# Elementwise work of both scan directions ahead of the scores, and PSUM readers ordered four dense blocks behind their matmuls

## The chip, the cores and the metric

The kernel runs on one core of one Trainium2 chip. The metric is device time in microseconds (us) of one execution. "Before" is the kernel as it was, "after" the changed one.

## The reference

The program is one inference step of a bidirectional backbone over 128 context tokens and 1024 latent tokens, width 1024: a SwiGLU feed-forward half step, a token-mixing block, and a second feed-forward half step. The change lies in the mixing block, whose heart is an RWKV-7 scan per direction and head:

```python
def rwkv7_scan(r, w, k, v, kk, a, s0, reverse):
    def step(S, inp):
        r_t, w_t, k_t, v_t, kk_t, a_t = inp
        sa = jnp.einsum('bhij,bhj->bhi', S, -kk_t)
        S = (S * w_t[:, :, None, :]
             + sa[..., None] * (kk_t * a_t)[:, :, None, :]
             + v_t[..., None] * k_t[:, :, None, :])
        return S, jnp.einsum('bhij,bhj->bhi', S, r_t)
...
    kk = k_h * p['k_k'].astype(f32).reshape(H, N)
    kk = kk * lax.rsqrt(jnp.sum(kk * kk, -1, keepdims=True) + 1e-12)
...
    y = ys[0] + ys[1]
    mean = jnp.mean(y, -1, keepdims=True)
    var = jnp.var(y, -1, keepdims=True)
    y = ((y - mean) * lax.rsqrt(var + EPS_GN)).reshape(B, T, D_RWKV)
```

Beside the scan stand large projections of the same hidden state (`h @ p['w_in']`, 5632 columns wide), which the scan needs only in part: r, k and v; the rest (g, the convolution's inputs, two gates) is read after it.

## The kernel before

**Dense work.** Each projection is three tiles of 384 tokens by 128 columns. A tile is eight blocks of three matmuls (lines 740 to 742: float32 as high and low parts), all into a PSUM tile `pj` (tag "mm", two buffers). The generator `proj` yields after every block, so a "dense block" is three matmuls of 128x384. All projections from the second group of heads on stand in one generator, `filler`, of 984 blocks, that is 2952 matmuls. With the 216 matmuls of the first group there are 3168 `pj` matmuls.

**The scan.** It is cut into 18 items: for g = 0 and 1 (four heads each) eight items of latents, both directions at once, and two items of context. Item i has a `front` (`stage_b` for each direction d: loads of `ops` and `sg`, exponentials, the products `BK` and `E`, the score matmuls `scr` of line 1047 and their masks, the transposed operand `bkt`), a `solve` (a small triangular solve: mostly DVE, lines 1079 to 1109, then the matmuls `l` of line 1116 and `l64b`), and a `seq` of two steps (lines 1165 to 1199). The loop issues `front(i+1)`, `seq(i)`, `solve(i+1)` at the highest priority, and then `fill(GI)`, which takes 40 blocks from `filler`. TensorE (PE) has one queue, in program order; a list scheduler writes that order ahead of time, chain work first where it is ready.

**Side jobs.** Three lanes run beside: `stage_k` makes the normalised key kk, `stage_v` turns v, `finish` normalises the output. A job is a generator too. Its yields are counted in dense blocks (`GL` 16, `GC` 14, `GM` 6, `GF` 8), and `PB` orders its instructions behind the block (`PB.anchor`) at which it was resumed. A job's small matmul (`cps`, `kkb`, `bon`, `vt`, `gv`) writes the one PSUM buffer of tag "oc", and its reader on DVE or ACT is issued at the same resumption. Before an item is issued, `need` takes further blocks from `filler`, one by one, until the side products of that item are issued:

```python
def need(kind, g, *bs):
    while not all((kind, 2 * g + pp, b) in made for b in bs for pp in range(2)):
        fill(1)
```

When `filler` is empty, `fill` still counts, and no matmul is issued. A full `pj` tile is read on ACT (`fso`, `ccs`, `xcs`) by `evict`, called two blocks into the next tile (`k == 1`).

After the last item the branch stage (`pb`, `pa`) loads what `finish` stored.

Of the kernel before, what the change touches and what calls it, by code (L numbers as in the profile page):

```python
# [10 lines left out]
F32 = mybir.dt.float32  # L11
F32R = mybir.dt.float32r
I32 = mybir.dt.int32
AF = mybir.ActivationFunctionType
# [46 lines left out]
def body(ctx: ExitStack, tc: tile.TileContext, I: dict, y_prompt, y_sample, new_state):  # L61
# [173 lines left out]

    def rsq(ps, n, scale, eps):
        x = tiny.tile([128, 16], F32, name="nx", tag="nx")[:, :n]
        V.tensor_scalar(out=x, in0=ps[:, :n], scalar1=scale, scalar2=eps, op0=ALU.mult, op1=ALU.add)
        return newton(x, n)

    def compact(sq, n, rhs, nr, scale, eps, tag="sc", PE=PE):
# [3 lines left out]
        return rsq(ps, n * nr, scale, eps)  # L245

# [412 lines left out]
def mixer(nc, tc, pool, env):  # L659
# [68 lines left out]
    def proj(col, evac, ts=range(NT)):  # L728

        if col not in ahead:  # L730
            assert not plan or plan[0] == col
            if plan:
                fetch()
            else:
                ahead[col] = load_w(w_in[:, col:col + 128], 8, G)
        w = ahead.pop(col)
        for t in ts:
            ps = e.psp.tile([128, TW], F32, name="pj", tag="mm")
            for k, ((hi, lo), (xh, xl)) in enumerate(zip(w, hx(t))):
                PE.matmul(ps, lo, xh, start=(k == 0), stop=False)  # L740
                PE.matmul(ps, hi, xl, start=False, stop=False)  # L741
                ins = PE.matmul(ps, hi, xh, start=False, stop=(k == 7))  # L742
                clock["dense"] += 1
                if k == 0 and t == ts[0]:
                    fetch(ins)
                if k == 5 and t == ts[len(ts) > 1]:
                    for job in halves:
                        job()
                    halves.clear()
                if k == 1:  # L750
                    evict()
# [47 lines left out]
    with ExitStack() as ph:  # L799
# [6 lines left out]

        SG = [st.tile([128, 4, 65], F32, name=f"sg{d}") for d in range(2)]
        YS = st.tile([128, 256], F32, name="ys")
        YL = st.tile([128, 4, 2, 256], F32, name="yl")
        ZV = [st.tile([128, 4, 2, 128], F32, name=f"zv{i}") for i in range(4)]  # L810
        UB = [st.tile([128, 2, 128], F32, name=f"ub{i}") for i in range(2)]
        for t_ in SG:
            G.memset(t_[:, :, 0:1], 0.0)
        for t_ in UB + [YS]:
            G.memset(t_, 0.0)
        HR = [slice(0, 64), slice(64, 128)]

        GI, GF, GL, GM, GC, SG_ = 40, 8, 16, 6, 14, 2
        def job_g(p):
# [120 lines left out]


        def stage_k(p, t0, n, bon=True):

# [18 lines left out]
            yield 3  # L962
            rs = compact(a, nt, sel, 2, 1.0, 1e-12, "oc", PB)
            yield GC
            ps = ps_.tile([128, 256], F32, name="kkb", tag="oc", bufs=1)[:, :n]
            for i in range(nt):
                for h in range(2):
                    PB.matmul(ps[HR[h], i * 128:(i + 1) * 128], rs[:, 2 * i + h:2 * i + h + 1].to_broadcast([128, 64]), ident, start=True, stop=True)
            kk = a
            V.scalar_tensor_tensor(out=kk, in0=k, scalar=e.KK_[:, p:p + 1], in1=ps, op0=ALU.mult, op1=ALU.mult)  # L970
            for h, dst in enumerate(mirrored(p, 4, 1, t0, n)):
                SP.dma_start(dst, kk[HR[h]])
            made.add(("kk", p, (t0 - NCTX) // 256))
            yield 4
            ps = ps_.tile([128, 256], F32, name="bon", tag="oc", bufs=1)[:, :n]
            PB.matmul(ps, bones, b, start=True, stop=True)
            o = v
            V.tensor_tensor(out=o, in0=v, in1=ps, op=ALU.mult)
            S.activation(out=o, in_=o, func=AF.Identity, bias=gb4[:, p:p + 1])
# [3 lines left out]
        def stage_v(p, t0, n, zv):  # L983


            nb = n // 64
            while ("rkv", p) not in made:
                yield 1
            v = oload(vd[p], t0, n, "lv", PB.first)
            yield GL  # L990
            ps = ps_.tile([128, 4, 64], F32, name="vt", tag="oc", bufs=1)
            for i in range(nb):
                for h in range(2):
                    hr, kr = HR[h], HR[1 - h]
                    PB.matmul(ps[kr, i], v[hr, i * 64:i * 64 + 64], cent[hr] if t0 >= NCTX else ident[hr, hr], start=True, stop=True)
            for h in range(2):
                S.activation(out=zv[HR[1 - h], 0:nb, p % 2, HR[h]], in_=ps[HR[1 - h], 0:nb], func=AF.Copy)
            made.add(("vt", p, (t0 - NCTX) // 256))
# [14 lines left out]
        def stage_b(g, d, t0, A, it):  # L1013
# [9 lines left out]
            c3 = "p (s t) -> p s t"  # L1023
            Fd = q1.tile([128, 4, 65], F32, name="ff", tag="ff")[:, :nb]
            S.activation(out=Fd, in_=sg, func=AF.Exp, scale=-CDEC)
            Gd = q1.tile([128, 4, 65], F32, name="fl", tag="fl")[:, :nb]
            S.activation(out=Gd, in_=sg, func=AF.Exp, scale=CDEC)
            if d == 0:
# [12 lines left out]
            mk = masks[d].unsqueeze(1).to_broadcast([128, nb, 128])  # L1041
            pst, pse = (ps_.tile([128, 4, 128], F32, name="scr", tag="sc") for x in range(2))
            for i in range(nb):
                for own, ps in ((1, pst), (0, pse)):
                    for h in range(2):
                        o = h if own else 1 - h
                        PE.matmul(ps[64 * o:64 * o + 64, i], BK[64 * h:64 * h + 64, o, i * 64:i * 64 + 64], E[64 * h:64 * h + 64, s0 + i, h], start=True, stop=True)  # L1047
            V.tensor_tensor(out=TT[:, s0:s0 + nb], in0=pst[:, :nb], in1=mk, op=ALU.mult)
            for h in range(2):
                kr = slice(64 - 64 * h, 128 - 64 * h)  # L1050
                S.activation(out=E[kr, s0:s0 + nb, h], in_=pse[kr, :nb], func=AF.Copy)
                G.tensor_tensor(out=E[kr, s0:s0 + nb, h], in0=E[kr, s0:s0 + nb, h], in1=mk[kr], op=ALU.mult)
            N = A["N"][:, 0] if d == 0 else q1.tile([128, 4, 32], F32, name="nt_", tag="nt_")
            for h in range(2):
                for b_ in range(2):
                    S.activation(out=N[quad(h, b_)], in_=TT[quad(h, b_), s0:s0 + nb, 32 * b_:32 * b_ + 32], func=AF.Copy)
            if d:
                V.transpose(out=A["N"][:, 1], in_=N)
            ps = ps_.tile([128, 4, 128], F32, name="bkt", tag="sc")
            for i in range(nb):  # L1060
                for x in range(2):
                    PE.matmul(ps[HR[x], i], BK[:, x, i * 64:i * 64 + 64], ident, start=True, stop=True)
            S.activation(out=BT[:, s0:s0 + nb], in_=ps[:, :nb], func=AF.Copy)

# [142 lines left out]
        def finish(p, t0, n, y):  # L1207
# [6 lines left out]
            yo = y  # L1214
            if t0 < NCTX:
                ps = ps_.tile([128, 256], F32, name="gm", tag="oc", bufs=1)[:, :n]
                PB.matmul(ps, bones, y, start=True, stop=True)
                V.scalar_tensor_tensor(out=yc, in0=ps, scalar=-1.0 / 64, in1=y, op0=ALU.mult, op1=ALU.add)
                yo = yc
            a = q1.tile([128, 256], F32, name="ysq", tag="f4")[:, :n]  # L1220
            PB.first(S.activation(out=a, in_=yo, func=AF.Square))
            yield GM
            rs = compact(a, nt, sel, 2, 1.0 / 64, 64e-5, "oc", PB)
            yield GC
            ps = ps_.tile([128, 256], F32, name="gv", tag="oc", bufs=1)[:, :n]
# [3 lines left out]
            V.tensor_tensor(out=yc, in0=yo, in1=ps, op=ALU.mult)  # L1229
            V.scalar_tensor_tensor(out=yc, in0=yc, scalar=gg4[:, p:p + 1], in1=bv, op0=ALU.mult, op1=ALU.add)  # L1230
# [292 lines left out]
```

## Time and profile before

| | us |
|---|---|
| median of 3 runs | 3232.46 (3229.34 to 3234.77) |
| profiled execution, its own time | 3226.22 |
| span of that execution (first to last instruction) | 3224.3 |
| mean granted TensorE clock | 0.962 |

The rows below come from the profiled execution. Its span lacks 1.9 us that lie around it, and its time is 6.2 us under the median of the runs. Feed-forward and projections fill roughly the first 1080 us and the last 1070 us; the scan with its beginnings and its tail lies between.

### The profile page before, as it was taken

What the parts mean: (1) busy time and instruction counts of PE and PEld (TensorE: products, weight loads), DVE (VectorE), ACT (ScalarE), POOL (GpSimd) and SP (SyncE); (2) the same over time, 40 slices, a digit from 0 to 9 for tenths busy, and PEclk for the clock granted to TensorE, in tenths of its full rate; (3) what the DMA queues carried; (4) which work ended last, traced back from release to release, by engine and by line L of the source; (5) the groups of instructions that cost most, each with busy time, mean ns of one, the idle gap of its engine ahead of it and who ended that gap; (6) DMA issues with size and microseconds to landing.
All of it is one profiled execution on the core that took longest, in us unless ns stands there. A gap on an engine that the chain in (4) does not pass through costs nothing.

```text
span 3224.3 us, 55042 instructions
## 1 busy us (share of the span) xinstructions
PE 3005.2 (93%) x21284; PEld 2836.3 (88%) x21284; DVE 1821.8 (57%) x4148; ACT 1151.7 (36%) x2618; POOL 453.8 (14%) x436
## 2 busy tenths in 40 slices
PE   8999999999989989988898898679989999999998
PEld 5999999999979987877777777469989999999998
DVE  7535655654875344566875668665782323323356
ACT  5421121113545424354544445332543111121244
POOL 1000000000241121333322322100220000000012
PEclk9999999999989999999999999779989999999999
DMA  8422333324534542322333223236432111111244
GB/s 271 148 63 85 111 89 92 99 79 126 163 118 133 178 132 66 111 81 79 90 114 105 88 86 108 62 112 190 141 99 66 46 38 49 46 38 45 84 144 131
DMA packets 483898, 330.80 MB, mean 103 GB/s; under 512 B 49768, under 2 KB 461748, under 8 KB 483636
## 3 DMA queue, kind: packets, MB, share of 16 engines
q1 hardware_dynamic: 483008, 326.80, 33.9%
q8 instruction: 167, 2.74, 0.4%
q14 instruction: 95, 0.78, 0.1%
q10 hardware_dynamic: 308, 0.44, 0.0%
q0 software_dynamic: 320, 0.04, 0.0%
HBM read 265.58 MB, written 61.60 MB: 101 GB/s over the span
## 4 chain that ended last, share of the span: by engine, by line
PE 69%; DVE 17%; ACT 5%; issue 4%; DMA 3%; POOL 1%; SPq 0%; DVEq 0%; ACTq 0%; POOLq 0%
PE po L220 6%; PE po L219 6%; PE po L221 6%; PE pg L220 5%; PE pg L219 5%; PE pg L221 5%; PE pu L220 5%; PE pu L219 5%; PE pu L221 5%; PE pj L742 3%; PE pj L740 3%; PE pj L741 3%; DVE un L1088 2%; PE scr L1047 2%; DMA ops<-opd 1%
## 5 line engine op out<-in xcount | busy, mean ns | idle before, releaser
L138 ACT ACTIVATE whi<-wst 128x512 fp32r<-128x512 f32 (+1 forms) x578 | 350.4, 611 | 731.6 <-PE po L221 393.1
L139 DVE TENSOR_TENSOR wlo<-wst,whi 128x512 fp32r<-128x512 f32 (+1 forms) x480 | 326.7, 681 | 305.4 <-ACT whi L138 296.1
L740 PE MATMUL pj<-hh,wlo 128*128 128x384 f32 x1056 | 375.4, 355 | 0.3 <-ACT fso L768 0.3
L741 PE MATMUL pj<-hl,whi 128*128 128x384 f32 x1056 | 371.1, 351 | 2.7 <-POOL hl L269 1.4
L742 PE MATMUL pj<-hh,whi 128*128 128x384 f32 x1056 | 371.3, 352 | 0.0
L220 PE MATMUL pg<-hl,whi 128*128 128x384 f32 x1056 | 356.8, 338 | 5.3 <-POOL hl L269 2.9
L219 PE MATMUL po<-ah,wlo 128*128 128x384 f32 x1056 | 357.1, 339 | 3.8 <-ACT ah L138 3.8
L219 PE MATMUL pg<-hh,wlo 128*128 128x384 f32 x1056 | 357.7, 339 | 1.9 <-DVE wlo L139 1.3
L220 PE MATMUL po<-al,whi 128*128 128x384 f32 x1056 | 356.3, 338 | 0.4 <-DVE al L139 0.4
L221 PE MATMUL pg<-hh,whi 128*128 128x384 f32 x1056 | 356.1, 337 | 0.0
L221 PE MATMUL po<-ah,whi 128*128 128x384 f32 x1056 | 355.7, 337 | 0.0
L219 PE MATMUL pu<-hh,wlo 128*128 128x384 f32 x1056 | 355.4, 337 | 0.0
L220 PE MATMUL pu<-hl,whi 128*128 128x384 f32 x1056 | 354.0, 335 | 0.0
L221 PE MATMUL pu<-hh,whi 128*128 128x384 f32 x1056 | 354.0, 335 | 0.0
L279 POOL TENSOR_TENSOR ss<-ss,sqt 128x384 f32<-128x384 f32 x78 | 88.7, 1140 | 1695.8 <-ACT sqt L278 1691.3
L432 DVE TENSOR_TENSOR sil<-sil,pu 128x384 f32<-128x384 f32 x132 | 72.8, 552 | 352.7 <-PE pu L221 352.6
L404 DVE TENSOR_TENSOR o<-o,po 128x384 f32<-128x384 f32 x288 | 159.0, 552 | 172.4 <-PE po L221 171.4
L741 PEld LDWEIGHTS pj<-hl,whi 128*128 128x128 f32 x1056 | 204.3, 193 | 9.9 <-issue 3.0
L740 PEld LDWEIGHTS pj<-hh,wlo 128*128 128x128 f32 x1056 | 203.7, 193 | 10.4 <-issue 5.7
L742 PEld LDWEIGHTS pj<-hh,whi 128*128 128x128 f32 x1056 | 204.2, 193 | 7.4 <-issue 3.3
L220 PEld LDWEIGHTS pg<-hl,whi 128*128 128x128 f32 x1056 | 200.1, 189 | 7.8 <-DVE hl L271 3.9
L219 PEld LDWEIGHTS po<-ah,wlo 128*128 128x128 f32 x1056 | 198.6, 188 | 4.8 <-ACT ah L138 4.8
(584 smaller groups left out, 5746.9 us busy)
## 6 DMA issues: line engine op xcount, KB each, us to landing
wst<-in_ffn_w SPq DMA_DIRECT2D x324, 256.0 KB, 2.9
wmod<-in_w_mod SPq DMA_DIRECT2D x144, 256.0 KB, 2.8
wst<-in_w_in SPq DMA_DIRECT2D x94, 256.0 KB, 3.3
ops<-opd SPq DMA_DIRECT2D x36, 640.0 KB, 4.5
wst<-in_ffn_w SPq DMA_DIRECT2D x96, 192.0 KB, 2.5
xo<-xd SPq DMA_DIRECT2D x64, 192.0 KB, 3.9
wst<-in_w_out SPq DMA_DIRECT2D x48, 256.0 KB, 2.8
opd<-zv SPq DMA_DIRECT2D x24, 384.0 KB, 2.8
```

The source lines that it names most:

```text
L138: first(S.activation(out=hi, in_=src, func=AF.Copy))
L139: eng.tensor_tensor(out=lo, in0=src, in1=hi.bitcast(F32), op=ALU.subtract)
L219: PE.matmul(ps, lo, xh, start=(k == 0), stop=False)
L220: PE.matmul(ps, hi, xl, start=False, stop=False)
L221: later.tick(PE.matmul(ps, hi, xh, start=False, stop=(k == nk - 1)))
L279: eng.tensor_tensor(out=ssum, in0=ssum, in1=q, op=ALU.add)
L404: V.tensor_tensor(out=O[m][t], in0=O[m][t], in1=ps, op=ALU.add)
L432: V.tensor_tensor(out=s, in0=s, in1=pu, op=ALU.mult)
L740: PE.matmul(ps, lo, xh, start=(k == 0), stop=False)
L741: PE.matmul(ps, hi, xl, start=False, stop=False)
L742: ins = PE.matmul(ps, hi, xh, start=False, stop=(k == 7))
L1047: PE.matmul(ps[64 * o:64 * o + 64, i], BK[64 * h:64 * h + 64, o, i * 64:i * 64 + 64], E[64 * h:64 * h + 64, s0 + i, h], start=True, stop=True)
```

## The change

Four edits. (1) `stage_b` is split: it does the loads, exponentials and products of its direction and returns `scores`; `front` calls both directions' first parts and then both `scores`. The buffers `ff` and `fl`, shared by the directions, go: one exponential is written to a static tile per direction (`sf`), the other in place over `sg`, whose first column is now 1 instead of 0. (2) In the side jobs the reader of a small matmul is issued four yields (`GV`) after it, and ordered behind the block reached by then. (3) `take` holds the "oc" buffer for one job at a time, from the matmul to its reader; a job that finds it held comes back 7 blocks later. (4) `evict` is called four blocks into the next tile (`k == 3`).

```diff
-                if k == 1:
+                if k == 3:
                     evict()
...
+        SF = [st.tile([128, 4, 65], F32, name=f"sf{d}") for d in range(2)]
...
-        for t_ in SG:
-            G.memset(t_[:, :, 0:1], 0.0)
+        for t_ in SG + SF:
+            G.memset(t_[:, :, 0:1], 1.0)
...
-        GI, GF, GL, GM, GC, SG_ = 40, 8, 16, 6, 14, 2
+        GI, GF, GL, GM, GC, SG_, GV = 40, 8, 16, 6, 14, 2, 4
...
+        held = []
+        def take():
+            while held:
+                yield 7
+            held.append(1)
+
         def stage_k(p, t0, n, bon=True):
...
-            rs = compact(a, nt, sel, 2, 1.0, 1e-12, "oc", PB)
+            yield from take()
+            ps = e.sums(a, nt, sel, 2, "oc", PB)
+            yield GV
+            rs = e.rsq(ps, 2 * nt, 1.0, 1e-12, PB.first)
+            held.clear()
             yield GC
+            yield from take()
             ps = ps_.tile([128, 256], F32, name="kkb", tag="oc", bufs=1)[:, :n]
...
-            V.scalar_tensor_tensor(out=kk, in0=k, scalar=e.KK_[:, p:p + 1], in1=ps, op0=ALU.mult, op1=ALU.mult)
+            yield GV
+            PB.first(V.scalar_tensor_tensor(out=kk, in0=k, scalar=e.KK_[:, p:p + 1], in1=ps, op0=ALU.mult, op1=ALU.mult))
+            held.clear()
...
-            Fd = q1.tile([128, 4, 65], F32, name="ff", tag="ff")[:, :nb]
-            S.activation(out=Fd, in_=sg, func=AF.Exp, scale=-CDEC)
-            Gd = q1.tile([128, 4, 65], F32, name="fl", tag="fl")[:, :nb]
-            S.activation(out=Gd, in_=sg, func=AF.Exp, scale=CDEC)
+            Fd, Gd = SF[d], sg
+            S.activation(out=Fd[:, :, 1:65], in_=sg[:, :, 1:65], func=AF.Exp, scale=-CDEC)
+            S.activation(out=Gd[:, :, 1:65], in_=sg[:, :, 1:65], func=AF.Exp, scale=CDEC)
...
-            if g < 2:
-                stage_b(g, 0, NCTX + j * 128, A[i], i)
-                stage_b(g, 1, NCTX + (7 - j) * 128, A[i], i)
-            else:
-                for d in range(2):
-                    stage_b(j, d, 0, A[i], i)
+            at = [(g, NCTX + j * 128), (g, NCTX + (7 - j) * 128)] if g < 2 else [(j, 0)] * 2
+            for f in [stage_b(gg, d, t0, A[i], i) for d, (gg, t0) in enumerate(at)]:
+                f()
```

`bon`, `vt`, `gv` and the sums of `finish` get the same `take`, `yield GV` and `PB.first`.

What this does to the order of the `pj` matmuls can be counted. `need` takes 170, 140, 0 and 50 blocks ahead of items 0, 2, 9 and 10 in the kernel before, and 229, 198, 60 and 130 in the changed one; everywhere else `fill(GI)` takes its 40. In the written order of PE, so many of the 3168 `pj` matmuls stand ahead of the end of each item's `l` matmuls:

| item | 0 | 1 | 2 | 3 | 4 | 5 | 6 | 7 | 8 | 9 | 10 | 11 | 12 | 13 | 14 | 15 | 16 | 17 |
|---|---|---|---|---|---|---|---|---|---|---|---|---|---|---|---|---|---|---|
| before | 882 | 955 | 1419 | 1549 | 1668 | 1803 | 1925 | 2041 | 2150 | 2238 | 2525 | 2641 | 2756 | 2879 | 3005 | 3129 | 3168 | 3168 |
| after | 1058 | 1136 | 1780 | 1894 | 2022 | 2146 | 2263 | 2369 | 2481 | 2807 | 3168 | 3168 | 3168 | 3168 | 3168 | 3168 | 3168 | 3168 |

The first place is PE's queue around the solve of item 15 (`l`; `cps`, `gv`, `kkb`, `vt`, `bon` are side jobs' small matmuls, `yp` is the scan's step). Before:

```order
L741 MATMUL pj<-hl_1_8842,whi 128x384
L742 MATMUL pj<-hh_1_8841,whi 128x384
L1116 MATMUL l_20892<-xr,ab_20604 32x32 x2
L740 MATMUL pj<-hh_1_8867,wlo 128x384
L741 MATMUL pj<-hl_1_8868,whi 128x384
L742 MATMUL pj<-hh_1_8867,whi 128x384
L1116 MATMUL l_20892<-xr,ab_20605 32x32 x2
```

The same place of the changed kernel's PE queue, where line 1116 has become line 1144:

```order
L1205 MATMUL yp<-e_20302,zv_9437 64x64 x4
L177 MATMUL cps<-cst,ysq 128x2 x2
L177 MATMUL cps<-cst,oa 128x2
L177 MATMUL gv<-cst,ny 64x128 x4
L177 MATMUL kkb<-cst,ny 64x128 x2
L177 MATMUL vt<-cst,lv 64x64 x4
L177 MATMUL bon<-od,cst 128x128
L177 MATMUL cps<-cst,ysq 128x2 x2
L1144 MATMUL l_20580<-xr,ab_20296 32x32 x2
```

The dense matmuls that stood before and within the solve are gone from this place; small matmuls of side jobs follow each other without a block between.

The second place is DVE's queue behind the transpose that opens a solve in the middle of the scan (`un` is the solve, `ops` and `e` are the next item's products, `zv` the running step). Before:

```order
L1088 TENSOR_TENSOR un<-lm,x_14773 128x24
L1039 TENSOR_TENSOR e_15076<-ops,ff 64x4x64
L1040 TENSOR_TENSOR e_15076<-ops,ff 64x4x64
L1039 TENSOR_TENSOR e_15076<-ops,ff 64x4x64
L1040 TENSOR_TENSOR e_15076<-ops,ff 64x4x64
L1184 COPY zv_9436<-sq 64x2x64
L1184 COPY zv_9435<-sq 64x2x64
L1039 TENSOR_TENSOR e_15077<-ops,fl 64x4x64
```

And in the changed kernel:

```order
L1060 TENSOR_TENSOR ops<-ops,sf_9433 128x512
L1063 TENSOR_TENSOR e_15517<-ops,sf_9432 64x4x64
L1064 TENSOR_TENSOR e_15517<-ops,sf_9432 64x4x64
L1063 TENSOR_TENSOR e_15517<-ops,sf_9432 64x4x64
L1064 TENSOR_TENSOR e_15517<-ops,sf_9432 64x4x64
L1063 TENSOR_TENSOR e_15518<-ops,sg_9431 64x4x64
L1064 TENSOR_TENSOR e_15518<-ops,sg_9431 64x4x64
L1063 TENSOR_TENSOR e_15518<-ops,sg_9431 64x4x64
L1064 TENSOR_TENSOR e_15518<-ops,sg_9431 64x4x64
L1212 COPY zv_9438<-sq 64x2x64
```

Both kernels have the products of both directions in the same stretch of the solve; the first product now stands ahead of them and all eight stand in a row, ahead of the step's copies. The masks of the scores stand behind the solve in both kernels.

## Rows read from the trace of the kernel before

**Rows 1.** The page: busy time and share of each engine.

```profile
PE 3005.2 (93%) x21284; PEld 2836.3 (88%) x21284; DVE 1821.8 (57%) x4148; ACT 1151.7 (36%) x2618; POOL 453.8 (14%) x436
```

**Rows 2.** Windows cut at items' first L1116 instruction: each engine's busy time, clock, DMA.

```profile
core 0: us, PE busy (x) PEld busy (x) DVE busy (x) ACT busy (x) POOL busy (x), PEclk, DMA share, GB/s
1083.30:1212.10 128.80, 117.33 (x752) 110.53 (x750) 47.29 (x110) 35.33 (x78) 31.25 (x24) 0.94 0.45 131
1253.60:1371.30 117.70, 109.64 (x843) 99.96 (x842) 57.73 (x151) 41.33 (x101) 36.95 (x32) 0.94 0.36 104
...
2015.50:2054.50 39.00, 23.92 (x362) 19.73 (x362) 26.83 (x92) 14.47 (x39) 8.75 (x10) 0.85 0.33 100
2054.50:2093.10 38.60, 23.23 (x358) 18.34 (x358) 28.68 (x102) 15.74 (x47) 6.22 (x8) 0.72 0.07 21
2093.10:2156.50 63.40, 42.20 (x338) 33.21 (x338) 35.50 (x127) 20.50 (x53) 1.15 (x4) 0.67 0.33 94
...
1371.30:1662.90 291.60, 253.49 (x2845) 216.02 (x2845) 209.56 (x614) 138.27 (x383) 100.05 (x98) 0.95 0.31 90
1662.90:1788.00 125.10, 112.19 (x1147) 96.98 (x1147) 77.91 (x216) 54.81 (x152) 32.26 (x30) 0.95 0.36 104
1788.00:2093.10 305.10, 251.44 (x3036) 211.32 (x3036) 214.70 (x687) 144.65 (x417) 79.99 (x84) 0.91 0.29 86
```

**Rows 3.** The same windows, instructions that touch `pj` alone (PE, PEld, ACT).

```profile
1083.30:1212.10 128.80, 105.65 (x562) 98.69 (x562) 11.29 (x23) 0.94 0.45 131
1253.60:1371.30 117.70, 90.75 (x465) 81.18 (x464) 9.32 (x19) 0.94 0.36 104
...
2054.50:2093.10 38.60, 0.00 (x0) 0.00 (x0) 0.00 (x0) 0.72 0.07 21
...
1371.30:1662.90 291.60, 158.54 (x735) 128.81 (x735) 15.12 (x31) 0.95 0.31 90
1662.90:1788.00 125.10, 76.31 (x372) 64.03 (x372) 7.87 (x16) 0.95 0.36 104
1788.00:2093.10 305.10, 136.18 (x646) 109.88 (x646) 13.20 (x27) 0.91 0.29 86
```

**Rows 4.** A window in which PE runs `pj` matmuls alone, columns as in rows 3.

```profile
1274.90:1287.20 12.30, 12.30 (x72) 12.03 (x70) 1.48 (x3) 1.00 0.54 161
```

**Rows 5.** DVE in order of time, around the end of item 16's solve.

```profile
2054.51 0.45 DVE L1109 STREAM_TRANSPOSE xr<-xr 128x256 f32<-128x256 f32 x1
...
2059.75 0.69 DVE L1048 TENSOR_TENSOR ab<-scr,cst 128x512 f32<-128x512 f32 x1 [4.75 <-PE scr L1047]
...
2065.12 0.69 DVE L1048 TENSOR_TENSOR ab<-scr,cst 128x512 f32<-128x512 f32 x1 [2.63 <-PE scr L1047]
...
2069.27 1.25 DVE L1079 STREAM_TRANSPOSE lm<-nn 128x1024 f32<-128x1024 f32 x1
```

**Rows 6.** Waits over the whole program: us in total, times, longest us.

```profile
DVE ab L1048 <- PE scr L1047: 104.4, 30, 6.5
ACT fso L768 <- PE pj L742: 94.1, 40, 4.5
DVE nx L238 <- PE cps L177: 71.0, 30, 8.3
...
DVE oa L970 <- PE kkb L177: 36.4, 9, 5.9
...
DVE or L978 <- PE bon L177: 21.7, 11, 2.9
```

**Rows 7.** The chain that ended last, behind the last item: start, us, what.

```profile
2112.98 0.30 DVE yc__22273 L1218
...
2124.50 0.30 DVE yc__22306 L1218
...
2129.97 0.30 DVE yc__22339 L1218
...
2132.16 0.69 PE pb L220
```

More of the change, by code (lines that the diff above doesn't have):

```diff
@@ L234, in newton, with rsq, sums @@
         return y
-    def rsq(ps, n, scale, eps):
+    def rsq(ps, n, scale, eps, first=lambda ins: None):
         x = tiny.tile([128, 16], F32, name="nx", tag="nx")[:, :n]
-        V.tensor_scalar(out=x, in0=ps[:, :n], scalar1=scale, scalar2=eps, op0=ALU.mult, op1=ALU.add)
+        first(V.tensor_scalar(out=x, in0=ps[:, :n], scalar1=scale, scalar2=eps, op0=ALU.mult, op1=ALU.add))
         return newton(x, n)
-    def compact(sq, n, rhs, nr, scale, eps, tag="sc", PE=PE):
+    def sums(sq, n, rhs, nr, tag="sc", PE=PE):
         ps = psp.tile([128, 16], F32, name="cps", tag=tag, bufs=1 if tag == "oc" else 2)
@@ L244, in compact @@
             PE.matmul(ps[:, i * nr:(i + 1) * nr], sq[:, i * 128:(i + 1) * 128], rhs, start=True, stop=True)
-        return rsq(ps, n * nr, scale, eps)
+        return ps
+    def compact(sq, n, rhs, nr, scale, eps, tag="sc", PE=PE):
+        return rsq(sums(sq, n, rhs, nr, tag, PE), n * nr, scale, eps)
     def bcast(rs, sp, PE=PE):
@@ L974, in stage_k @@
             yield 4
+            yield from take()
             ps = ps_.tile([128, 256], F32, name="bon", tag="oc", bufs=1)[:, :n]
@@ L977, in stage_k @@
             o = v
-            V.tensor_tensor(out=o, in0=v, in1=ps, op=ALU.mult)
+            yield GV
+            PB.first(V.tensor_tensor(out=o, in0=v, in1=ps, op=ALU.mult))
+            held.clear()
             S.activation(out=o, in_=o, func=AF.Identity, bias=gb4[:, p:p + 1])
@@ L990, in stage_v @@
             yield GL
+            yield from take()
             ps = ps_.tile([128, 4, 64], F32, name="vt", tag="oc", bufs=1)
@@ L995, in stage_v @@
                     PB.matmul(ps[kr, i], v[hr, i * 64:i * 64 + 64], cent[hr] if t0 >= NCTX else ident[hr, hr], start=True, stop=True)
+            yield GV
             for h in range(2):
-                S.activation(out=zv[HR[1 - h], 0:nb, p % 2, HR[h]], in_=ps[HR[1 - h], 0:nb], func=AF.Copy)
+                PB.first(S.activation(out=zv[HR[1 - h], 0:nb, p % 2, HR[h]], in_=ps[HR[1 - h], 0:nb], func=AF.Copy))
+            held.clear()
             made.add(("vt", p, (t0 - NCTX) // 256))
@@ L1040, in stage_b @@
                 V.tensor_tensor(out=E[hr, s0:s0 + nb, h, 64:128], in0=r[hr].rearrange(c3, t=64), in1=fr[hr], op=ALU.mult)
[L1041 to L1063, printed above, removed]
+            def scores():
+                mk = masks[d].unsqueeze(1).to_broadcast([128, nb, 128])
+                pst, pse = (ps_.tile([128, 4, 128], F32, name="scr", tag="sc") for x in range(2))
+                for i in range(nb):
+                    for own, ps in ((1, pst), (0, pse)):
+                        for h in range(2):
+                            o = h if own else 1 - h
+                            PE.matmul(ps[64 * o:64 * o + 64, i], BK[64 * h:64 * h + 64, o, i * 64:i * 64 + 64], E[64 * h:64 * h + 64, s0 + i, h], start=True, stop=True)
+                V.tensor_tensor(out=TT[:, s0:s0 + nb], in0=pst[:, :nb], in1=mk, op=ALU.mult)
+                for h in range(2):
+                    kr = slice(64 - 64 * h, 128 - 64 * h)
+                    S.activation(out=E[kr, s0:s0 + nb, h], in_=pse[kr, :nb], func=AF.Copy)
+                    G.tensor_tensor(out=E[kr, s0:s0 + nb, h], in0=E[kr, s0:s0 + nb, h], in1=mk[kr], op=ALU.mult)
+                N = A["N"][:, 0] if d == 0 else q1.tile([128, 4, 32], F32, name="nt_", tag="nt_")
+                for h in range(2):
+                    for b_ in range(2):
+                        S.activation(out=N[quad(h, b_)], in_=TT[quad(h, b_), s0:s0 + nb, 32 * b_:32 * b_ + 32], func=AF.Copy)
+                if d:
+                    V.transpose(out=A["N"][:, 1], in_=N)
+                ps = ps_.tile([128, 4, 128], F32, name="bkt", tag="sc")
+                for i in range(nb):
+                    for x in range(2):
+                        PE.matmul(ps[HR[x], i], BK[:, x, i * 64:i * 64 + 64], ident, start=True, stop=True)
+                S.activation(out=BT[:, s0:s0 + nb], in_=ps[:, :nb], func=AF.Copy)
@@ L1065, in quad @@
+            return scores
         def quad(h, b):
@@ L1215, in finish @@
             if t0 < NCTX:
+                yield from take()
                 ps = ps_.tile([128, 256], F32, name="gm", tag="oc", bufs=1)[:, :n]
@@ L1219, in finish @@
                 yo = yc
+                held.clear()
             a = q1.tile([128, 256], F32, name="ysq", tag="f4")[:, :n]
@@ L1222, in finish @@
             yield GM
-            rs = compact(a, nt, sel, 2, 1.0 / 64, 64e-5, "oc", PB)
+            yield from take()
+            ps = e.sums(a, nt, sel, 2, "oc", PB)
+            yield GV
+            rs = e.rsq(ps, 2 * nt, 1.0 / 64, 64e-5, PB.first)
+            held.clear()
             yield GC
+            yield from take()
             ps = ps_.tile([128, 256], F32, name="gv", tag="oc", bufs=1)[:, :n]
@@ L1228, in finish @@
                     PB.matmul(ps[HR[h], i * 128:(i + 1) * 128], rs[:, 2 * i + h:2 * i + h + 1].to_broadcast([128, 64]), ident, start=True, stop=True)
-            V.tensor_tensor(out=yc, in0=yo, in1=ps, op=ALU.mult)
+            yield GV
+            PB.first(V.tensor_tensor(out=yc, in0=yo, in1=ps, op=ALU.mult))
+            held.clear()
             V.scalar_tensor_tensor(out=yc, in0=yc, scalar=gg4[:, p:p + 1], in1=bv, op0=ALU.mult, op1=ALU.add)
```

## The prediction

> **What bounds the kernel now.** I read the page first: PE is busy 93% of the span, DVE 57%, ACT 36% [rows 1]. So the program as a whole is PE's, and work that is only late on DVE or ACT costs nothing until PE waits for it. Then I cut the scan at each item's first `l` matmul and read the windows twice, for all engines and for the dense matmuls (`pj`) alone. They fall into three kinds. Where `need` pours in dense blocks, PE is nearly full: 117.3 of 128.8 us ahead of item 0, 109.6 of 117.7 us between items 1 and 2, 112.2 of 125.1 us between items 8 and 10 [rows 2]. In the ordinary items PE is busy 253.5 of 291.6 us (items 2 to 8) [rows 2], and 158.5 us of that are dense matmuls [rows 3]. At the end there is none left: from item 16 to 17 not one `pj` matmul runs [rows 3], PE is busy 23.2 of 38.6 us at a granted clock of 0.72, and DVE 28.7 us [rows 2].
>
> Compare an item with dense work and one without: items 10 to 17 take 305.1 us, 43.6 us each, and carry 646 `pj` matmuls [rows 2, 3]; the item without any takes 38.6 us [rows 2]. A dense matmul alone on PE costs 12.3 us / 71 = 0.173 us [rows 4] (the window touches 72, the first and last in part). The 92 of an item are thus 16 us of PE time, and the item is only 5 us longer for them. Dense work under the scan costs about a third of its price; beside `need` it costs all of it.
>
> **The change part by part.** *Where the blocks go.* Each reader now comes 4 blocks after its matmul, and `take` sends rivals for the buffer away for 7 blocks at a time. `need` waits for these jobs in blocks, so it takes 229, 198, 60 and 130 of them in place of 170, 140, 0 and 50, 257 more. `filler` has no more blocks than before: it now runs empty at item 10, where it ran empty at item 16. The counts of `pj` matmuls ahead of each solve, which stand with the change, give the shifts, at 0.173 us each:
>
> - ahead of item 0: 1058 for 882, 176 more: +30.4 us
> - items 0 to 1: 5 more: +0.9 us
> - items 1 to 2: 644 for 464, 180 more: +31.1 us
> - items 2 to 8: 701 for 731, 30 fewer: -5.2 us
> - items 8 to 10: 687 for 375, 312 more: +54.0 us
>
> Together +111.2 us. These stretches are PE's own (rows above), so I take the full price; the gaps that could swallow some are a term of their own below.
>
> The Trainium skill ("TensorE: Matmul & The Clock Gate", Back-to-back issue gap) gives N/2.4 + 2.5 ns for one isolated matmul at the upper clock, an estimate of 162.5 ns for 384 columns. By it the +111.2 us would be about +104 us, 7 us less; the trace's 0.173 us differs and decides.
>
> *What comes back.* Items 10 to 17 lose all their 643 matmuls. Each interval then resembles the one from item 16 to 17. The rows of its DVE show what is left: from the solve's last transpose (2054.5) to the next opening one (2069.3) are 14.8 us, with waits of 4.75 and 2.63 us for the score matmuls; the rest of the item is the solve itself, on DVE [rows 5]. I take 38 us, a little under 38.6 since evictions and weights are gone: 7 x 38 = 266 for 305.1, -39 us. Bounds: 7 x 35 = 245 (-60 us), 35 being the 38.6 less half the 7.4 us of those waits; and 43.6 as now (0 us).
>
> *Readers, evictions.* The waits aimed at are real: DVE waits 71.0 us for `cps`, 36.4 for `kkb`, 21.7 for `bon`, ACT 94.1 us for `pj` [rows 6]. But they are waits for PE, at moments when PE has other work; what they can give back is at most the time that PE stands idle. Through item 10 that is 11.5 + 8.1 + 38.1 + 12.9 = 70.6 us (the windows less their PE busy time [rows 2]). Most of it is the chain's own latency, and an ordinary item's jobs now spread over more items; I take a quarter, -18 us, bounds 0 and -71. The later eviction has two more blocks to wait, 6 x 0.173 = 1.0 us, and the second `pj` buffer covers it: a tile is 24 x 0.173 = 4.2 us, so 2.1 us are left from the fourth block to the tile's end. If that cover failed, PE would wait for ACT; no row shows such a wait now, and I take 0 (to +10 us, a tenth of ACT's 94.1 reversed).
>
> *Both directions first.* The static `sf` and `sg` remove nothing from DVE's count. The score masks wait 104.4 us for PE [rows 6], but the written order has them behind the solve before and after, so I take 0. Against it: the first product now stands before the eight others, and waits for GpSimd and the `ops` load ahead of the solve. Bounds: 0, and a gain or loss of at most one such mask wait, 3.5 us an item (104.4 / 30), which the ends above and below already span.
>
> What is queued behind the later readers: the stores of kk on SP's queue, and behind these the `ops` load of the item's `front`. They come 8 blocks later in each `stage_k` (two `GV`), which is just what `need` now waits out in blocks, so this wait is in the +111.2 us already. The in-place exponential adds one more: the next item's `sg` load on SP, with the loads and stores queued behind it, now waits for the products of the item before instead of its exponentials. These products run within the first third of the solve, an item ahead of the load's use, so the price is 0 as long as an item is some 38 us long.
>
> *The tail.* After the last item, `finish` jobs run one after another, with a single buffer for their loads. Before, four (context) are left; in the changed order three more matmul groups (`cps`, `gv`) of `finish` stand behind the last solve. Consecutive jobs start 11.5 and 5.5 us apart (2113.0, 2124.5, 2130.0), and the dense branch follows at 2132.2 [rows 7]. Three more cost 3 x 5.5 to 3 x 11.5, 16 to 35 us; part runs beside the last two steps, so I take +15, bounds +8 and +35.
>
> Sum: 111.2 - 39 - 18 + 15 = +69 us. On the profiled 3226.2 us that is 3295 us. The median of the runs stands 6.2 us above that execution; I add it: **3302 us**, 2.1% slower.
>
> **The rivals.**
>
> *B, the bare items give nothing back.* Without dense work the granted clock is 0.72 and, in the tail, 0.67 [rows 2]; side jobs stand in PE's queue back to back, so their readers wait where they are issued. If each bare item stays at 43.6 us, 39 us are not returned: 3341 us, and with the long tail 3361. For it: side work of four context keys and eight outputs falls into these items. Against: the item from 16 to 17 had the low clock already and two `finish` jobs, and took 38.6 us. The Trainium skill ("TensorE: Matmul & The Clock Gate", The HAM clock gate) has the clock at half rate after idle time; by that rule bare items stay near the lower level throughout. The granted 0.72 agrees in part only.
>
> *C, the waits were the path.* If the waits of side readers had each been on the chain, their removal would be worth 71.0 + 36.4 + 21.7 = 129 us [rows 6] in place of 18: 111.2 - 39 - 129 + 15 = -42 us, 3191 us, faster. It decides from 111.2 - 39 + 15 = 87 us of waits on the path. Against it: PE idles 70.6 us through item 10, all causes together, and the chain cannot outrun PE there.
>
> *D, nothing moves.* If the order had not changed where it counts, the time would be within 0.2% (6.5 us; runs of one kernel spread by 5.4 us, so less than that is no measurable change). The counts speak against it: the blocks are moved in the written program.
>
> **How the numbers follow.** The forecast with its neighbourhood, 3270 to 3330: 0.58. B and the long tail, 3330 to 3375: 0.22. Larger gains by short waits or bare items near 35 us, 3239 to 3270: 0.11. D: 0.03. C: 0.06. The ends of all terms together would be 3232 + 111 - 60 - 71 + 8 = 3220 and 3232 + 111 + 35 + 10 = 3388, but they are not met at once. The range 3255 to 3355 leaves out C, D, half of the small gains and the upper half of B, 2 in 10. Faster 0.06, same 0.03, slower 0.91.
>
> **What would show it.** In the profile after: the last `pj` matmul stands ahead of item 10's solve, and the windows from item 10 to 17 hold none, with a granted clock of 0.6 to 0.8 and 36 to 40 us an item; item 0's `l` comes about 25 to 30 us later and item 10's about 90 us later than now; the waits of `nx`, `oa` and `or` on PE shrink to a fraction; the stretch from the last solve to steady `pb` grows from 63 to some 75 us. I am wrong in the size of the gain if the items 2 to 8 shorten by more than 3 us each; wrong in the give-back if bare items take under 35 or over 42 us; wrong altogether if the chain reaches item 10 at today's time, which would mean that PE had room for the blocks.

## The result and the profile after

The changed kernel takes 3365.91 us (median of 4 runs, 3360.41 to 3370.67), the kernel before beside it 3233.61 us: ratio 1.041, 95% interval [1.0394, 1.0426]. It is slower by 132 us, where I had forecast 69, and stands 11 us above the top of my range. The direction and the place were right, the size was not. The profiled execution took 3360.41 us, its span is 3358.5 us.

First the page, busy time and share of each engine, answering to [rows 1]:

```profile
PE 3029.0 (90%) x21284; PEld 2869.7 (85%) x21284; DVE 1816.1 (54%) x4148; ACT 1147.5 (34%) x2618; POOL 454.5 (14%) x438
```

PE does the same 21284 matmuls; 134 us were added to the span and only 24 to PE's busy time. So PE now stands idle where it did not before. To find where, the windows cut at the items' first `l` matmul (line 1116 has become 1144), columns as in [rows 2]. They are: ahead of item 0, items 1 to 2, 2 to 8, 8 to 10, the end of that one by itself, 10 to 17, and from item 17 to the first `pb`:

```profile
1083.30:1234.10 150.80, 139.42 (x907) 133.10 (x907) 47.23 (x111) 39.43 (x87) 36.59 (x28) 0.98 0.41 118
1276.00:1431.80 155.80, 142.07 (x1036) 131.78 (x1036) 66.67 (x164) 49.66 (x119) 53.22 (x47) 0.94 0.29 85
1431.80:1705.50 273.70, 247.26 (x2722) 210.26 (x2723) 186.01 (x533) 128.29 (x363) 86.38 (x88) 0.92 0.33 94
1705.50:1917.50 212.00, 178.51 (x1568) 158.85 (x1569) 98.52 (x311) 72.24 (x191) 40.76 (x36) 0.91 0.36 108
1881.40:1917.50 36.10, 8.53 (x68) 6.09 (x70) 27.45 (x81) 7.88 (x20) 6.76 (x5) 0.53 0.50 141
1917.50:2208.20 290.70, 150.71 (x2344) 123.45 (x2345) 191.46 (x610) 118.17 (x363) 58.51 (x68) 0.61 0.15 41
2208.20:2266.30 58.10, 27.37 (x276) 20.66 (x276) 28.02 (x126) 8.69 (x31) 1.14 (x4) 0.53 0.16 46
```

The `pj` matmuls alone in four of these windows, answering to [rows 3]:

```profile
1083.30:1234.10 150.80, 129.21 (x709) 122.37 (x707) 14.19 (x29) 0.98 0.41 118
1276.00:1431.80 155.80, 122.99 (x646) 113.06 (x646) 12.72 (x26) 0.94 0.29 85
1705.50:1917.50 212.00, 136.29 (x692) 119.83 (x691) 14.12 (x29) 0.91 0.36 108
1917.50:2208.20 290.70, 0.00 (x0) 0.00 (x0) 0.00 (x0) 0.61 0.15 41
```

Against [rows 2, 3] this gives the account of the 134 us of span, beside my terms. The columns before and after are lengths of windows; the line from item 17 runs to the end of the span.

| stretch | before | after | difference | my term |
|---|---|---|---|---|
| ahead of item 0 | 128.8 | 150.8 | +22.0 | +30.4 |
| items 0 to 1 | 41.5 | 41.9 | +0.4 | +0.9 |
| items 1 to 2 | 117.7 | 155.8 | +38.1 | +31.1 |
| items 2 to 8 | 291.6 | 273.7 | -17.9 | -5.2 |
| items 8 to 10 | 125.1 | 212.0 | +86.9 | +54.0 |
| items 10 to 17 | 305.1 | 290.7 | -14.4 | -39 |
| item 17 to the end | 1131.2 | 1150.3 | +19.1 | +15 |
| waits removed, wherever | | | | -18 |

Two rows carry the miss: items 8 to 10, 33 us dearer than I had them, and items 10 to 17, which gave back 14 us for 39.

The last `pj` matmul ends at 1881.4, and item 10's `l` starts at 1917.5. In between PE is busy 8.5 of 36.1 us. The chain of waits through that stretch, in order of time (start, us, what; a few of its pieces):

```profile
1881.70 0.45 SPq L1046
1882.20 0.68 SPq L1046
1882.93 2.04 SPq L1027
1885.01 4.15 DMA f<-bvd
1889.18 1.51 DVE e L1064
1890.70 0.37 SPq L1045
1891.12 2.16 DMA sg<-opd
...
1900.55 0.42 DVE e L1063
1900.97 1.40 DVE e L1064
1902.37 0.60 DVE ops L1060
...
1916.98 0.41 DVE xr L1136
1917.45 0.43 DVE xr L1137
1917.93 0.64 PE l L1144 x28
```

The reader is to see loads on SP's queue first, then the front's products, then the solve on DVE, up to `l`: no dense matmul is left that could stand beside it. The waits of the same stretch (us in total, times, longest) name the late loads of `ops` and `sg`:

```profile
POOL ops L1059 <- DMA ops<-opd: 29.8, 3, 25.1
ACT sf L1050 <- DMA sg<-opd: 10.5, 1, 10.5
```

I had also said that the waits of `nx`, `oa` and `or` would shrink to a fraction. Over the whole program they grew, against [rows 6]:

```profile
DVE ab L1074 <- PE scr L1073: 110.3, 29, 7.2
DVE nx L238 <- PE cps L177: 89.8, 35, 11.8
DVE oa L988 <- PE kkb L177: 67.0, 10, 8.5
DVE or L999 <- PE bon L177: 35.5, 12, 4.3
```

They are no sign of time on the path. Cut by stretch, most of `oa` and `or` and much of `nx` stand ahead of item 2, where `need` pours in blocks and DVE has little else to do (the first window of these waits, after):

```profile
DVE oa L988 <- PE kkb L177: 54.8, 7, 8.5
DVE nx L238 <- PE cps L177: 40.0, 6, 11.8
...
DVE or L999 <- PE bon L177: 30.1, 8, 4.3
```

In the ordinary items 2 to 8, where I had looked for their price, the kernel before had only this:

```profile
DVE nx L238 <- PE cps L177: 3.1, 4, 1.6
DVE or L978 <- PE bon L177: 2.8, 2, 1.5
```

and the kernel after has 1.2 us of `nx` there. Rival C, which wanted 129 us of such waits on the path, had no more than 6 us in these items.

### The profile page after: what moved, and what is told of

It reads as the page before. It is cut to its first block, busy times and chain, and to the rows that moved or that the text cites. A ratio compares the mean times of both kernels' runs of the same rounds, so it can differ in the third digit from the quotient of the medians.

```text
span 3358.5 us, 55083 instructions
## 1 busy us (share of the span) xinstructions
PE 3029.0 (90%) x21284; PEld 2869.7 (85%) x21284; DVE 1816.1 (54%) x4148; ACT 1147.5 (34%) x2618; POOL 454.5 (14%) x438
## 4 chain that ended last, share of the span: by engine, by line
PE 71%; DVE 17%; ACT 4%; DMA 3%; issue 3%; POOL 2%; SPq 0%; DVEq 0%; ACTq 0%; POOLq 0%
PE po L220 6%; PE po L219 6%; PE po L221 6%; PE pg L220 5%; PE pg L221 5%; PE pg L219 5%; PE pu L220 5%; PE pu L219 5%; PE pu L221 5%; PE pj L743 4%; PE pj L744 4%; PE pj L745 4%; DVE un L1116 3%; PE scr L1073 2%; DMA ops<-opd 1%
## 5 line engine op out<-in xcount | busy, mean ns | idle before, releaser
L743 PEld LDWEIGHTS pj<-hh,wlo 128*128 128x128 f32 x1056 | 203.9, 193 | 12.9 <-issue 7.8
L219 PEld LDWEIGHTS pg<-hh,wlo 128*128 128x128 f32 x1056 | 200.4, 190 | 2.4 <-DVE wlo L139 1.6
```

## The experiments

Two theories went into the first four runs. **A**: the loss is the early use of the dense blocks, nothing else. **B**: a good part of it lies in the readers or the new front themselves. All ratios are against the kernel before on the same chip.

**e1, only the blocks taken earlier.** The kernel before, with

```diff
         need("kk", 0, 0, 3)
+        fill(229 - clock["now"])
...
+            fill(max(0, {1: 467, 8: 807, 9: 977}.get(i, 0) - clock["now"]))
             with chain():
```

> The kernel before with none of the four edits; extra dense blocks are taken ahead of items 0, 2, 9 and 10, so that as many as in the changed kernel are gone by then (229, 467, 807 and 977) and the filler runs empty at item 10. Theory A (the loss is the early use of the blocks alone): 3345 to 3370 us, first l of item 0 some 20 to 25 us later than before, no pj matmul behind about 1880 us, items 10 to 17 bare at 41 to 42 us each. Theory B (a good part of the loss is in the readers or in the front that does both directions first): clearly less than the changed kernel, under 3330 us.

Measured 3280.24 us, 1.0147 [1.0132, 1.0162]: a third of the loss. Theory A in this form fell, and the time is one that theory B allowed. The trace says why. Of `pj` matmuls 875 stand ahead of item 0's `l`, as in the kernel before (880), not 1056: the extra blocks were taken when the job that the chain waits for was already issued, so the scheduler could put the chain ahead of them. Between items 1 and 2 and between 8 and 10 the same holds in part (612 and 549 `pj` matmuls for 646 and 691). Blocks taken early cost as far as the job that is waited for stands behind them.

**e2, the readers alone** (edits 2 and 3; front, buffers and evict as before):

> The kernel before with edits 2 and 3 alone (readers four yields later, the oc buffer held); front, sf/sg and evict as before. Theory A: the same as the changed kernel, 3355 to 3375 us, since the blocks are taken as in it (229, 198, 60, 130). Theory B, in the form that the front or the later evict costs: 20 us or more under the changed kernel, 3345 us or less.

3365.49 us, 1.0406 [1.039, 1.0423]: the whole loss. The front and the later evict add none of it.

**e3, all but the readers** (edits 1 and 4):

> The changed kernel without edits 2 and 3 (no GV, no take): both directions first, sf static, sg in place, evict four blocks into the next tile; blocks are taken as in the kernel before. Theory A: no change, 3225 to 3245 us. Theory B, in the form that the front costs at item 10 (36.9 us without a dense matmul): slower, 3255 us or more. If both directions first frees PE of the score masks' waits (104.4 us over 30): faster, under 3220 us.

3218.09 us, 0.9958 [0.9944, 0.9973]: 14 us faster than before, better than either theory had it; only the side remark on the score masks' waits allowed it, and e8 does not bear that out. Both edits were at 0 in my sum.

**e4, readers four yields later, other gaps shorter by as much.** The changed kernel, with

```diff
-        GI, GF, GL, GM, GC, SG_, GV = 40, 8, 16, 6, 14, 2, 4
+        GI, GF, GL, GM, GC, SG_, GV = 40, 4, 12, 6, 10, 2, 4
...
             while held:
-                yield 7
+                yield None
...
-            if self.cur is None or clock["now"] < self.at:
+            if self.cur is None or clock["now"] < self.at or self.stuck and held:
```

where `stuck` is set by a yield of None.

> The changed kernel with its readers still four yields behind their matmuls, but with the other gaps of the jobs shortened by as much (GL 12, GC 10, GF 4) and a job that finds the oc buffer held resumed when it is free instead of 7 blocks later: 179, 146, 0 and 100 blocks are taken ahead of items 0, 2, 9 and 10 (before 170, 140, 0, 50; changed 229, 198, 60, 130), and the filler runs empty at item 14. Theory A: near the kernel before, 3230 to 3265 us. Theory B, in the form that later readers cost by themselves: 3290 us or more. If later readers give back what I summed as waits removed (18 us), under 3225 us.

3253.55 us, 1.0063 [1.0051, 1.0075], within theory A's range. So the readers stand behind four blocks and 111 of the 132 us are gone, as soon as the jobs are hardly longer (`need` takes 425 blocks, 360 before). A gain by the readers themselves does not show here.

From these four I formed **theory L**: what costs is the length of a side job, counted in blocks. In the changed kernel each `stage_k` is longer by three `GV` of 4, and by 7 for each time that it finds the buffer held. `need` waits it out with blocks that stand ahead of the chain, wherever in the job the readers are.

**e5, longer gaps, no edit at all.** The kernel before, with

```diff
-        GI, GF, GL, GM, GC, SG_ = 40, 8, 16, 6, 14, 2
+        GI, GF, GL, GM, GC, SG_ = 40, 14, 20, 22, 20, 2
```

> The kernel before with none of the four edits, but longer gaps in the side jobs (GL 20, GC 20, GF 14, GM 22 for 16, 14, 8, 6), so that need takes about as many blocks as in the changed kernel (227, 472, 800 and 973 gone ahead of items 0, 2, 9 and 10 for 229, 467, 807 and 977). Readers stand at the resumption of their matmul, as before. Theory L (what costs is the length of a side job counted in blocks, wherever its readers stand): 3350 to 3380 us, as the changed kernel. Theory R (readers behind blocks cost by themselves): 3275 to 3310 us, near the run in which only blocks were taken earlier (3280).

3373.27 us, 1.043 [1.0413, 1.0448]. The loss is reproduced with every reader at its matmul's side. Theory L holds, and its rival, that the readers cost by themselves, is out.

**e6, need counts on without blocks.** The changed kernel, with

```diff
             for _ in range(n):
-                PB.anchor = next(filler, PB.anchor)
+                if not hold:
+                    PB.anchor = next(filler, PB.anchor)
```

and `hold` set while `need` runs from item 8 on.

> The changed kernel, but from item 8 on need counts on without taking blocks from the filler, so 190 blocks stay for later: 323 pj matmuls stand between the solves of items 8 and 10 for 687, and items 11 to 14 get 363. Theory L with PE as the price of need's blocks: items 8 to 10 shorter by about 364 x 0.173 = 63 us, items 10 to 17 longer by 5 to 15 us, 3300 to 3330 us. Rival (that stretch is the side jobs' own latency, the blocks only ride along): items 8 to 10 still over 190 us, 3350 us or more.

3285.63 us, 1.0168 [1.0154, 1.0182], 80 us less than the changed kernel and more than I expected. All engines, items 8 to 10 and 10 to 17:

```profile
1708.40:1832.80 124.40, 109.66 (x1171) 92.71 (x1170) 91.06 (x288) 55.75 (x158) 33.04 (x30) 0.96 0.39 112
1832.80:2129.00 296.20, 208.54 (x2716) 172.90 (x2716) 196.67 (x628) 131.97 (x393) 69.54 (x76) 0.78 0.25 70
```

Items 8 to 10 fell from 212.0 to 124.4 us, so the blocks set that stretch and not the side jobs' own latency. Items 10 to 17 rose by 5.5 us only, although 365 of the `pj` matmuls now run in them.

**e7, no readers, gaps shorter than before.** Edits 1 and 4, with

```diff
-        GI, GF, GL, GM, GC, SG_, GV = 40, 8, 16, 6, 14, 2, 4
+        GI, GF, GL, GM, GC, SG_, GV = 40, 4, 12, 4, 10, 2, 4
```

> The changed kernel without edits 2 and 3, and with shorter gaps in the side jobs (GL 12, GC 10, GF 4, GM 4): need takes 133, 92, 0 and 0 blocks ahead of items 0, 2, 9 and 10 (before 170, 140, 0, 50), and the filler lasts past item 17. Theory L, turned round: what need does not take costs a third or less under the scan. 112, 125 and some 140 pj matmuls fewer in the three stretches are 19 + 22 + 24 = 65 us, given back at a third to a half: 3160 to 3200 us. Rival (the stretches are the side jobs' own latency): 3205 to 3225 us, as the run without edits 2 and 3 (3218). Rival (small matmuls so close behind their inputs stop PE's queue): over 3225 us.

3170.07 us, 0.9806 [0.9791, 0.9821], as theory L has it: 48 us under e3 for 135 blocks fewer taken by `need`. Items 10 to 17, all engines and then `pj` alone:

```profile
1722.30:2024.20 301.90, 273.36 (x3182) 231.77 (x3182) 217.12 (x677) 146.25 (x422) 88.41 (x90) 0.96 0.30 88
```

```profile
1722.30:2024.20 301.90, 168.87 (x792) 137.24 (x792) 16.02 (x33) 0.96 0.30 88
```

These are the rows against which the bare items of the changed kernel are to be read: 792 dense matmuls and 11.2 us more, 0.014 us each, where one alone takes 0.173 us [rows 4]. The granted clock differs too, 0.96 here for 0.61 there; the last section comes back to it.

**e8, the front alone** (edit 1):

> The kernel before with edit 1 alone (both directions first, sf static, sg in place); evict two blocks into the next tile as before. If the 14 us that edits 1 and 4 together gave back are the front's: 3212 to 3224 us. If they are the later evict's: 3228 to 3238 us. My prediction had both at nothing.

3228.00 us, 0.9986 [0.9975, 0.9997]. **e10, the later evict alone** (edit 4, `k == 3`):

> The kernel before with edit 4 alone: a full pj tile is read four blocks into the next one for two. My prediction had it at 0 to +10 us. The front alone gave 3228 us and both together 3218, so if the two add up: 3218 to 3227 us. If the later evict helps only with the new front, or the difference was chance: 3228 to 3236 us. If PE waits for ACT, as my bound has it: 3238 us or more.

3225.46 us, 0.9985 [0.9973, 0.9998]. Each gives some 5 us, with an interval that is just clear of none; multiplied they make 0.9971, at the edge of what e3 measured for both. That they help a little together is shown, which of them does more is not.

**e9, all four edits, gaps shorter.** As e4, with `GL` 10, `GC` 7, `GF` 2, `GM` 4, `GV` 2.

> All four edits, with gaps so short (GL 10, GC 7, GF 2, GM 4, GV 2, a job that finds oc held resumed when it is free) that need takes 140, 88, 0 and 0 blocks, as in the run with short gaps and no readers (133, 92, 0, 0; 3170 us); pj matmuls ahead of the solves of items 0, 2 and 17 are 788, 1182 and 2934 for 772, 1178 and 2939. Theory L (only blocks count, readers nothing): 3160 to 3185 us. If the readers' waits for PE are worth the 18 us that I summed, with the same blocks: 3155 us or less. If readers behind blocks cost by themselves: 3190 us or more.

3152.03 us, 0.9753 [0.9735, 0.9771]: 78 us faster than before, the fastest of all, and 18 us under e7 with nearly the same blocks ahead of each solve. 11 of the 18 us stand where I had looked for them, in the ordinary items: items 2 to 8 take 284.1 us for e7's 295.2, with 743 `pj` matmuls for 736 (all engines; e9, then e7):

```profile
1327.20:1611.30 284.10, 250.64 (x2879) 214.66 (x2879) 204.49 (x636) 139.38 (x385) 100.22 (x98) 0.97 0.33 95
```

```profile
1329.70:1624.90 295.20, 260.35 (x2872) 221.82 (x2872) 213.34 (x637) 137.72 (x384) 98.02 (x96) 0.92 0.32 91
```

That readers behind blocks are worth something, if the job does not grow by them, is the likely reading. It is not shown: the gaps of the two runs are not the same.

**e11, gaps shorter still, no readers.** Edits 1 and 4 with `GI` 46, `GL` 8, `GC` 6, `GF` 2, `GM` 2, `SG_` 1:

> The run with short gaps and no readers taken further: GL 8, GC 6, GF 2, GM 2, a side step after each block (SG_ 1), and GI 46 so that the filler still ends with the scan; need takes 113, 46, 0 and 0 blocks. 61 and 80 pj matmuls fewer ahead of item 0 and between items 1 and 2 are 24 us by 0.173, given back at up to a half by more blocks per item: 3145 to 3162 us by theory L. Rival (the stretches have come down to the side jobs' own latency): 3163 to 3175 us, no change from 3170. Rival (small matmuls so close behind their inputs stop PE): over 3175 us.

3160.52 us, 0.9782 [0.976, 0.9803]. In theory L's range, but its interval overlaps that of e7. Items 1 to 2 fell from 99.3 to 85.6 us; part of it went into the item from 16 to 17, which took 66.3 us with 220 `pj` matmuls. PE was busy 62.0 us of them, so cover has a bound: in an item with that many blocks PE is the limit again.

**e12, the last blocks kept for item 10.** The changed kernel, with

```diff
-                PB.anchor = next(filler, PB.anchor)
+                if not (hold and clock["now"] >= 984 - 42):
+                    PB.anchor = next(filler, PB.anchor)
```

and `hold` set while `need` runs.

> The changed kernel, but need leaves the last 42 blocks of the filler: it counts on without them ahead of item 10, and fill takes them behind item 9, so that they can stand beside the front and solve of item 10, which ran 36.9 us without a dense matmul. Blocks ahead of each solve are as many as in the changed kernel (2807 and 3168 at items 9 and 10). Theory I (part of the 87.7 us of items 8 to 10 is idle PE time beside item 10, since the filler ran empty just there): items 8 to 10 up to 42 x 3 x 0.173 = 22 us shorter, 3340 to 3355 us. Rival (items 8 to 10 cost what their blocks cost on PE, 0.173 each, wherever they stand): no change, 3360 to 3371 us.

3353.53 us, 1.0384 [1.037, 1.0398], 12 us under the changed kernel; the intervals just overlap. In its profiled execution items 8 to 10:

```profile
1711.70:1911.20 199.50, 176.60 (x1564) 157.72 (x1563) 97.51 (x297) 70.98 (x189) 40.92 (x35) 0.96 0.38 112
```

12.5 us less than in the changed kernel, with as many `pj` matmuls: PE's idle time there went from 33.5 to 22.9 us. So part of that stretch's cost was idle time beside item 10, about half of what these blocks could cover. The whole of that execution was no shorter, though: it took 3360.93 us, the slowest of its five, and the changed kernel's profiled one 3360.41. Items 10 to 17 took 6.5 us more, items 2 to 8 2.3 us more, and item 0's `l` came 3.7 us later. The gain in the stretch is shown; that it is the 12 us of the medians is not.

## Why the prediction missed the size

**What was right.** PE bounds the `need` stretches, and the shift of dense blocks ahead of the chain is the loss. Ahead of item 2 my terms sum to 62.4 us and 60.5 were measured. e5 makes the same loss with no edit, e6 takes most of it back. The last `pj` matmul stands ahead of item 10's solve, items 10 to 17 hold none, at a granted clock of 0.58 to 0.64 (0.6 to 0.8 was written down), and item 0's `l` came 22 us late for 25 to 30. Item 10's came 130 us late for 90. The tail's +15 was +19.1: more of `finish` is left behind item 17, as the chain shows, answering to [rows 7], and the first `pb` comes 59 us behind that item's `l` where it came 39 us behind it:

```profile
2225.63 0.43 DVE yc__22072 L1265
2236.58 0.49 DVE yc__22072 L1267
...
2240.57 0.40 DVE yc__22105 L1267
2267.18 0.69 PE pb L220
```

The front and the evict at 0 were small gains, 14 us together in e3; beside the long jobs they vanish (e2 against the changed kernel), and why was not tried. Two small slips of the working: the 70.6 us of idle time leave out items 0 to 1 (2.1 us), and what the range leaves out sums to a quarter, not to 2 in 10.

**One step that failed: "What comes back", -39 us, measured -14.4.** I took the item from 16 to 17, 38.6 us without dense work, for what items 10 to 16 would become. It is not typical of them: in the kernel before, in the changed one and in e7 it is the shortest of the seven. In the changed kernel the bare items take 39.1, 40.1, 43.4, 46.5, 43.9, 41.2 and 36.5 us, in e7, with all their cover, 43.3, 49.8, 41.8, 43.7, 45.9, 39.2 and 38.3. So the others are nearly as long without dense blocks, at the lower clock, as with them. Side work is not the whole reason: ten and eleven `cps` matmuls fall into the two longest, but none into the first three, one of them 43.4 us long, and the item that I took had eight, as the second row shows. What makes the others longer was not tried. `cps` alone, that item of the changed kernel and then, in the kernel before, the one that I took:

```profile
1996.70:2040.10 43.40, 0.00 (x0) 0.00 (x0) 0.00 (x0) 0.58 0.14 37
```

```profile
2054.50:2093.10 38.60, 1.21 (x8) 1.04 (x8) 0.30 (x2) 0.72 0.07 21
```

The first and the longest of the changed kernel's bare items, all engines:

```profile
1917.50:1956.60 39.10, 21.01 (x326) 17.34 (x326) 26.64 (x77) 17.89 (x56) 8.71 (x10) 0.59 0.20 54
...
2040.10:2086.60 46.50, 24.72 (x354) 20.40 (x354) 28.72 (x105) 18.45 (x55) 8.69 (x10) 0.61 0.15 42
```

The runs give the price that I lacked. Items 10 to 17 took, by `pj` matmuls in them: 0, 290.7 us (changed kernel), 294.5 (e5) and 297.2 (e12); 332, 305.2 (e1); 365, 296.2 (e6); 452, 300.8 (e4); 646, 305.1 (before [rows 2]); 792, 301.9 (e7); 794, 298.7 (e9). I wrote that dense work under the scan costs about a third of its price. Against the changed kernel it costs 0.010 (e9) to 0.022 us (before) a matmul, and 0.044 in e1, for the most part about a tenth of 0.173, so taking it away gives little back. The stretches without any differ by 6.5 us among themselves, so these prices are rough. Rival B, to which I gave 0.22, was the nearer reading: its items of 43.6 us were 41.5, and it named the lower clock. That its 3361 us came within 5 us of the result is luck, for 33 us of the way come from items 8 to 10, which it prices as I did.

**The larger one: items 8 to 10, priced at +54.0 as PE time alone, measured +86.9.** PE's busy time there rose by 178.5 - 112.2 = 66.3 us, 12 more than my term, and its idle time from 12.9 to 33.5 us, 20.6 more. 27.6 us of that idle time are in the 36.1 us between the last `pj` matmul and item 10's `l`. `need` had eaten the filler down to 7 blocks just ahead of that item, so its loads, front and solve ran with nothing beside them. The new front is not what makes this place slow: in e2, without it, 35.6 us pass between the same two points. I had counted how many blocks stand ahead of the solve, and not what is left beside it. e6, which kept 190 blocks for later, has 14.7 us of idle time in the stretch; e12 bears it out there for half of what it moved.

**Two terms that cannot be told apart as I wrote them: items 2 to 8, -5.2, and waits removed, -18.** Items 2 to 8 took 17.9 us less than before. That looks like the waits, and is mostly not: e5, with every reader at its matmul's side, took 15.7 us less there. DVE is busy 209.6 us in that stretch before [rows 2], and 186.0 and 185.5 us in the changed kernel and in e5: longer jobs put less side work into these items. e2, readers later at about the same job length, is 10.3 us under e5 there, and e9 11.1 us under e7, so some 10 us may be the readers'; the gaps differ in both pairs. All engines, items 2 to 8, e5 and then e2:

```profile
1444.30:1720.20 275.90, 244.96 (x2742) 207.06 (x2744) 185.53 (x528) 129.74 (x366) 85.86 (x85) 0.92 0.32 92
```

```profile
1439.90:1705.60 265.70, 238.10 (x2715) 202.28 (x2715) 188.83 (x533) 127.71 (x362) 86.59 (x87) 0.95 0.33 96
```

The sign that I named for the waits, the sums of `nx`, `oa` and `or`, was the wrong one: they grew, mostly where `need` keeps PE full.

**The price in one line.** Over before, e4, e5, e7 and the changed kernel `need` takes 360, 425, 613, 225 and 617 blocks. From before to e5 253 blocks cost 142 us, 0.56 us each; to the changed kernel 257 cost 132, 0.51 each; from e3 to e7 135 fewer gave 48 us, 0.36 each. Three matmuls are 0.52 us [rows 4]. Hidden under an item they cost 0.03 to 0.07, and 0.13 in e1.

## What to carry to other kernels

Where a wait is counted in filler work, each unit by which a job grows is paid at about full price at the point that waits for it, and the filler is missing later where it would have been nearly free. Shorten the job first and separate readers only within the same length; here that turned a loss of 132 us into a gain of 78, 61 of which came without later readers (e7). Shorter gaps with none of the four edits were not tried. To price work that runs under a latency-bound chain, compare the same stretch with and without it, not one stretch with another, and look at the clock of both; and read a sum of waits by stretch before it is taken for time on the path.

## What the chip showed unexpectedly

The granted clock of TensorE was 0.61 over items 10 to 17 without dense work, near the lower of its two levels (1.2 of 2.4 GHz), and 0.96 to 0.99 in the same items of e7 and e9, where PE was busy 273.4 of 301.9 and 265.5 of 298.7 us. Yet the slow-clocked stretch is the shorter one, by 11.2 and 8.0 us. That does not mean that the clock costs nothing. The scan's own score matmuls (`scr`) and the matmuls of its step that write `sq` are as many in both, and kept PE busy 77.5 us in the changed kernel and 56.1 in e9. Items 10 to 17, `scr` and then `sq` alone, the changed kernel:

```profile
1917.50:2208.20 290.70, 34.64 (x448) 27.74 (x448) 9.68 (x14) 16.55 (x28) 0.61 0.15 41
```

```profile
1917.50:2208.20 290.70, 42.89 (x544) 34.71 (x544) 31.61 (x130) 5.36 (x14) 0.61 0.15 41
```

The same in e9:

```profile
1710.00:2008.70 298.70, 25.97 (x448) 20.43 (x448) 9.67 (x14) 16.56 (x28) 0.99 0.31 91
```

```profile
1710.00:2008.70 298.70, 30.13 (x544) 23.48 (x544) 31.07 (x130) 5.36 (x14) 0.99 0.31 91
```

On the chain that ended last `scr` has 9.4% of the stretch in the changed kernel (27 us) and 5.2% in e9 (16 us), while the dense matmuls, 15.4% of e9's stretch (46 us), are gone from it. So it seems that what the chain got back from the dense matmuls it paid in part with slower matmuls of its own. This is read from two traces; no run holds the dense work fixed and changes the clock.

The Trainium skill ("TensorE: Matmul & The Clock Gate", The HAM clock gate) has two rates, half in an idle state and full in a busy one. The granted 0.61, over a stretch in which PE is busy 150.7 of 290.7 us, lies between them and near the half.
